# Norm factors behind the first products, first weights in halves, and a feed loop that splits its first loads

## The chip, the cores and the metric

The program runs on one core of a Trainium2 chip. The metric is the device time of one execution in microseconds, lower being better. The time given for a kernel is the median of its runs.

## The reference, cut to what matters

A sequence of 256 tokens with 1024 features passes through two layers and a second block. Layer 0 is retention and a squared-ReLU MLP, layer 1 an attention that selects blocks (here there is one block) and an MLP. The second block has four parallel branches under gates, a cross attention to a memory, and a gated feed-forward part. Each part reads `rms_norm(h, g_pre)` and adds `rms_norm(part(...), g_post)` to `h`.

```python
def rms_norm(x, g):
    xf = x.astype(jnp.float32)
    y = xf * lax.rsqrt(jnp.mean(xf * xf, axis=-1, keepdims=True) + NORM_EPS)
    return (y * g.astype(jnp.float32)).astype(x.dtype)
...
    q, k, v, g = jnp.split(h @ w_in, [H * DK, 2 * H * DK, 2 * H * DK + H * DV], axis=-1)
...
    o = o * lax.rsqrt(jnp.mean(o * o, axis=-1, keepdims=True) + NORM_EPS)
    o = o.transpose(0, 2, 1, 3).reshape(B, S, H * DV)
    o = o * jax.nn.silu(g.astype(jnp.float32))
    return o.astype(h.dtype) @ w_out
...
    for i in range(DEPTH):
        pre, post, w_in, w_out, mpre, mpost, w_up, w_down = layers[i]
        h = h + rms_norm(mixers[i % N_MIXERS](rms_norm(h, pre), w_in, w_out), post)
        h = h + rms_norm(sq_relu_mlp(rms_norm(h, mpre), w_up, w_down), mpost)
```

## The kernel before, in words

All weights are float32 and stream from memory once, as 203 chunks of 1 MB in the order of their use. A chunk comes in two pieces of 128x1024 (512 KB), which makes 406 pieces. Float32 products are made of float32r ones: a piece that has landed (`raw`) is split into `whi` (ScalarE, a copy, L156) and `wlo` (VectorE, the difference, L162), the activations into `xhi` and `xlo`, and `mm3` (L235 to L237) issues three products for each k-tile: hi by hi, hi by lo of the weights, lo by hi. The second of the three is the first that needs `wlo`.

The work of TensorE is cut into units. One unit takes one chunk with one token tile of 128 (there are two, t0 and t1) and is 12 products of 128x512, six on the chunk's first piece and six on its second; or it takes one chunk with all tokens and 24 products of 128x256. Behind each unit stands a call of `tick(n)`: it starts the split of up to n pieces (`prepare`), lets the background work (attention heads, activations) take one step, finishes the splits, and calls `feed()`, which issues loads on SyncE's queue until `nraw` pieces (5, and 3 at the end of a layer) are loaded ahead of their split. A piece counts as ready for a split two ticks after its load was issued, and at most `nprep` pieces (11 to 13) may be split ahead. If a unit comes to a chunk whose pieces have not been split, `weights()` splits them on the spot (`prepare(force=True)`).

The order of the program is the order of these calls; nothing is rescheduled. Every engine works its own instructions in that order and waits for what is not there yet.

At the end of each part stands `boundary`. Its last products take token tile 0 first, so that the norms of tile 0 run under the products of tile 1, and the norms of tile 1 under the next part's four (or three) units of token tile 0 (`fill0`). These units call `tick(2 * t)` with t = 0, so that they start no splits: in this stretch ScalarE and VectorE have the norm chain of tile 1, the evacuations of the units, and the transposed `xhi` and `xlo` of tile 1. U1, U2, U3 and U4 below are these four units in order; in front of U4 stand the transposes of tile 1.

There are five such boundaries with as_group units behind them: retention to MLP 0, MLP 0 to the block attention, that to MLP 1, MLP 1 to the second block, and cross attention to the feed-forward part. A sixth leads from the branches to the cross attention.

In front, `prenorm(h[0], g0, ...)` makes the normed tile 0 in token-major form, `to_T` transposes it on TensorE and splits it into `xhi` and `xlo`, and the first unit follows. The gain `gain_first` is loaded as a 128x1024 tile, the same row on all partitions.

These are the lines around which the change turns:

```python
    def feed(n=None):
        n = n or state["nraw"]
        while state["dma"] < min(npiece, state["prep"] + n):
            raw = b4([128, 1024], "raw")
            nc.sync.dma_start(raw, wall[state["dma"]])
            raws[state["dma"]] = raw, state["now"] + 2
            state["dma"] += 1
```

Of the kernel before, what the change touches and what calls it, by code (L numbers as in the profile page):

```python
# [24 lines left out]
# Newton steps for 1/sqrt on a scaled iterate: z -> (z*z*x - 3*c*c)*z maps c*y to -2*c^3*y'.  # L25
# [3 lines left out]
# columns of w_in_2  # L29
# [7 lines left out]
# columns of the per-partition parameter array  # L37
# [7 lines left out]
# columns of the row parameter array  # L45
# [21 lines left out]
    # retention rotary, transposed: [freq, pos]  # L67
# [4 lines left out]
    # partial rope, natural: [pos in tile, tile, cos cos | sin -sin]  # L72
# [15 lines left out]
# tiles of 4 KB a partition, for weights and data  # L88
NB4 = 43
# pieces that are loaded ahead of their split, and split ahead of their use, at the end of a layer  # L90
AHEAD = 3, 16
# products of the last layer behind its last activations
TAIL = 4
# pieces of weights that are split ahead, by phase
# [5 lines left out]
def tile_model(ctx: ExitStack, tc: tile.TileContext, order, wall, x, mem, gains, pparam, rparam, w_fg,  # L100
# [27 lines left out]
    # Chunks of 1 MB in the order of their use, in two pieces of 1024 columns. A piece lies in SBUF as loaded, and  # L128
    # then as two float32r parts, hi and lo, whose sum is the float32 value.
# [4 lines left out]
    def feed(n=None):  # L134
        n = n or state["nraw"]
        while state["dma"] < min(npiece, state["prep"] + n):
            raw = b4([128, 1024], "raw")
            nc.sync.dma_start(raw, wall[state["dma"]])
            raws[state["dma"]] = raw, state["now"] + 2
            state["dma"] += 1  # L140

    def waiting():
        """Pieces that can be split now: loads that were issued at least two ticks ago."""
        end = min(state["dma"], 2 * state["done"] + state["nprep"])
        return sum(raws[i][1] <= state["now"] for i in range(state["prep"], end))

    def prepare(n=1, force=False):
        """Start to split n pieces; the function that is returned does the rest of it."""
# [18 lines left out]
    def weights(key):  # L167
        """The two parts of the next chunk, each in two pieces."""
# [35 lines left out]
    def later(f):  # L204
        """Call f within the next tick but one."""
# [13 lines left out]
    def pipe(n, *stages, wait=0):  # L219
        """Stages (delay, f) of n items, one item a step; the later stages of earlier items go first."""  # L220
# [18 lines left out]
    def ws(o, w, c0, xh, xl, width=256):  # L239
        """o[feature, token] = w^T x; the chunk is [128][2048 / width][width]."""  # L240
# [5 lines left out]
    def as_(o, w, xh, xl, t, start, stop):  # L246
        """o[token, 512] += x w over the 4 k-tiles of a chunk [128][4][512]."""
# [5 lines left out]
    def down(acc, w, ah, al, t, start, stop):  # L253
        """acc[token, 1024] += a w over the 2 k-tiles of a chunk [128][2][1024]."""
# [18 lines left out]
    def rstd(ss, w, inv_d, name):  # L273
        """1/sqrt(ss*inv_d + eps), elementwise on [128, w]."""
# [28 lines left out]
    h = [cp.tile([128, D], F32, name=f"h{t}") for t in range(2)]  # L303
    HS = [slice(0, 512), slice(512, 1024)]
    g0 = b4([128, D], "gain_first")
    for t in range(2):
        for n in range(2):
            nc.sync.dma_start(h[t][:, HS[n]], x[0, tok(t), HS[n]])
        if t == 0:
            for n in range(2):  # L310
                nc.sync.dma_start(g0[:, HS[n]], gains[0:1, HS[n]].broadcast_to([128, 512]))
        feed(4 * t + 2)
# [12 lines left out]
    # the layer's input, transposed, in two parts of four k-tiles each  # L325
# [21 lines left out]
    def rms_scale(src, g, y, name):  # L347
        """y = src * g; returns 1/sqrt(mean(src^2) + eps), by ScalarE's square root and a Newton step in x' = 4x.
        Sources and results are pairs of halves."""
# [24 lines left out]
    def chain(acc, gp, gn, t, name, store=False, between=None):  # L374
        """h[t] += rms_norm(acc, gp); returns rms_norm(h[t], gn)."""
# [11 lines left out]
    def prenorm(src, gn, y, name):  # L387
        """y = rms_norm(src, gn)"""
# [51 lines left out]
    def as_group(specs, xh=xh2, xl=xl2):  # L440
        """specs: (keys of the two chunks, evacuate(t, psum)). Work of token tile 0, work of token tile 1."""
# [32 lines left out]
    def ws_units(key, evac, xh=xh, xl=xl, n=None):  # L474
        """The work of one chunk in two units."""
# [33 lines left out]
    def ret_vg_specs(hd):  # L509
# [3 lines left out]
        evacs = (lambda t, ps: split(rv[hd][0][:, t, :], rv[hd][1][:, t, :], ps),  # L513
                 lambda t, ps: nc.scalar.activation(rg[hd][:, t, :], ps, AF.Silu))
# [15 lines left out]
    def ret_attn(hd):  # L530
# [3 lines left out]
        for jt in range(2):  # L534
            o = ps[:, 0:256] if jt == 0 else ps[:, 256:384]
            for f in range(2):
                nc.tensor.matmul(o, qkT[:, 2 + f, tok(jt)], qkT[:, f, jt * 128:256], start=f == 0, stop=f == 1)
        pt = t2("pt")
        nc.vector.tensor_tensor(pt[:, 0:384], ps[:, 0:384], dec[hd // 2][:, (hd % 2) * 384:(hd % 2) * 384 + 384],
                                op=ALU.mult)  # L540
# [5 lines left out]
        for t in range(2):  # L546
# [5 lines left out]
            nc.scalar.activation(og, po, AF.Square, accum_out=ss)  # L552
            r = rstd(ss, 1, 1.0 / 512, "ret")
            nc.vector.scalar_tensor_tensor(og, po, r, g[:, t, :], op0=ALU.mult, op1=ALU.mult)
# [23 lines left out]

    load_sqrt()
    xn = prenorm(h[0], g0, b4([128, D], "xn0"), "f0")  # L580
    prepare(1, force=True)()
    new_x()
    to_T(xn, 0, xh2, xl2)
    prepare(1, force=True)()
    specs = ret_vg_specs(0)
    fill = as_group(specs[:1])
    fill[0][0]()
    prepare(2, force=True)()
    xn = b4([128, D], "xn1")
    r = rms_scale(two(h[1]), None, None, "f1")()  # L590
    for n in range(2):
        nc.vector.scalar_tensor_tensor(xn[:, HS[n]], h[1][:, HS[n]], r, g0[:, HS[n]], op0=ALU.mult, op1=ALU.mult)
    fill[0][1]()
    to_T(xn, 1, xh2, xl2)
    for f in fill[1]:
        f()
# [33 lines left out]
    def mlp_start(i):  # L630
        """The first 1024 features with tokens on the partitions, so that token tile 0 can go first."""
# [118 lines left out]
    def moba_n(hd):  # L750
        p = mp[hd]
        b, l, rl = mst.pop(hd)
        # the selected block is never a past one: each of its 256 weights is exp(NEG - m)
# [821 lines left out]
```

## Time and profile before

| what | value |
|---|---|
| time, median of 3 runs | 1275.82 us (1275.37 to 1276.14) |
| profiled execution, span | 1274.1 us |
| lies around the span, against the median | 1.7 us |
| TensorE busy | 1251.6 us, 98% of the span |
| VectorE busy | 877.6 us, 69% |
| ScalarE busy | 680.0 us, 53% |
| DMA | 227.43 MB, 179 GB/s |

The span is that of the profiled execution, the time that of runs without a profile. Busy times are means over a span with parts that have different limits; VectorE and ScalarE are far from full over the whole, and what they are at a given place is to be read there.

### The profile page before, as it was taken

How to read it: one execution, taken by the hardware profiler on the slowest of the kernel's cores; microseconds unless marked ns; L12 is line 12 of the kernel's file. 1: busy time of each engine (PE TensorE's matmuls, PEld its weight loads, DVE VectorE, ACT ScalarE, POOL GpSimd, SP SyncE). 2: the span in 40 equal slices, each digit the busy share in tenths (PEclk: the TensorE clock that was granted, in tenths of full speed). 3: DMA queues.
4: the chain of work that ended last, by engine and by line, in shares of the span. 5: the costliest groups of instructions: out<-in, count | busy, mean ns of one | idle time of the engine just before them, and what ended most of it. 6: DMA issues, size and time to landing. Idle time of an engine off the chain costs nothing.

```text
span 1274.1 us, 20056 instructions
## 1 busy us (share of the span) xinstructions
PE 1251.6 (98%) x7886; PEld 1123.7 (88%) x7886; DVE 877.6 (69%) x1540; ACT 680.0 (53%) x1104; POOL 9.3 (1%) x22
## 2 busy tenths in 40 slices
PE   6999999999999999999999999999999999999997
PEld 4888888899988888899988999889999897899996
DVE  5775768755556866765566677768877877588773
ACT  5553445644444755654453546555346565666552
POOL 0000000000000000000000000000000000000000
PEclk9999999999999999999999999999999999999999
DMA  9754464665564545566664644235566564465530
GB/s 346 270 186 158 153 226 154 215 203 185 183 207 150 183 136 176 182 210 188 196 202 163 215 133 149 67 118 180 183 182 203 190 220 165 150 191 185 187 116 34
DMA packets 64206, 227.43 MB, mean 179 GB/s; under 512 B 8048, under 2 KB 8304, under 8 KB 64112
## 3 DMA queue, kind: packets, MB, share of 16 engines
q1 hardware_dynamic: 61808, 217.76, 52.0%
q0 software_dynamic: 2304, 8.39, 1.9%
q8 instruction: 62, 1.02, 0.3%
q14 instruction: 32, 0.26, 0.1%
HBM read 225.08 MB, written 1.05 MB: 177 GB/s over the span
## 4 chain that ended last, share of the span: by engine, by line
PE 95%; DVE 2%; ACT 1%; issue 1%; DMA 1%; SPq 0%; DVEq 0%; ACTq 0%
PE ps_ws L235 13%; PE ps_ws L237 13%; PE ps_ws L236 13%; PE ps_as L237 6%; PE ps_as L235 6%; PE ps_as L236 6%; PE mlp L268 4%; PE mlp L267 4%; PE mlp L271 4%; PE ffn L268 1%; PE ffn L271 1%; PE ffn L267 1%; PE ps_br L235 1%; PE ps_br L237 1%; PE ps_br L236 1%; PE pt L294 1%
## 5 line engine op out<-in xcount | busy, mean ns | idle before, releaser
L162 DVE TENSOR_TENSOR wlo<-raw,whi 128x1024 fp32r<-128x1024 f32 x406 | 480.0, 1219 | 78.5 <-ACT whi L156 77.3
L156 ACT ACTIVATE whi<-raw 128x1024 fp32r<-128x1024 f32 x406 | 406.7, 1049 | 53.8 <-PE ps_ws L237 15.4
L235 PE MATMUL ps_ws<-xhi,whi 128*128 128x256 f32 x1376 | 391.6, 285 | 0.0
L236 PE MATMUL ps_ws<-xlo,whi 128*128 128x256 f32 x1376 | 389.3, 283 | 0.0
L237 PE MATMUL ps_ws<-xhi,wlo 128*128 128x256 f32 x1376 | 389.3, 283 | 0.0
L235 PEld LDWEIGHTS ps_ws<-xhi,whi 128*128 128x128 f32 x1376 | 263.8, 192 | 5.2 <-issue 3.7
L236 PEld LDWEIGHTS ps_ws<-xlo,whi 128*128 128x128 f32 x1376 | 263.9, 192 | 1.5
L237 PEld LDWEIGHTS ps_ws<-xhi,wlo 128*128 128x128 f32 x1376 | 263.8, 192 | 0.0
L235 PE MATMUL ps_as<-whi,xhi 128*128 128x512 f32 x352 | 142.6, 405 | 0.3 <-ACT xhi L231 0.2
L237 PE MATMUL ps_as<-whi,xlo 128*128 128x512 f32 x352 | 138.4, 393 | 0.1
L236 PE MATMUL ps_as<-wlo,xhi 128*128 128x512 f32 x352 | 138.1, 392 | 0.0
L268 PE MATMUL mlp<-wlo,act 128*128 128x512 f32 x240 | 93.7, 390 | 0.0
L267 PE MATMUL mlp<-whi,act 128*128 128x512 f32 x240 | 93.5, 390 | 0.0
L237 PEld LDWEIGHTS ps_as<-whi,xlo 128*128 128x128 f32 x352 | 66.4, 189 | 15.5 <-DVE xlo L232 1.2
L235 PEld LDWEIGHTS ps_as<-whi,xhi 128*128 128x128 f32 x352 | 66.6, 189 | 13.8 <-ACT xhi L231 1.1
L236 PEld LDWEIGHTS ps_as<-wlo,xhi 128*128 128x128 f32 x352 | 66.6, 189 | 13.6 <-DVE wlo L162 0.8
L662 DVE SCALAR_TENSOR_TENSOR relu<-ps_ws,relu 128x512 f32<-128x512 f32 x24 | 16.6, 691 | 87.1 <-ACT relu L661 87.1
L661 ACT ACTIVATE relu<-ps_ws 128x512 f32<-128x512 f32 x24 | 14.4, 598 | 113.8 <-PE ps_ws L237 113.8
L271 PE MATMUL mlp<-whi,act 128*128 128x512 f32 x240 | 74.0, 389 | 0.0
L271 PEld LDWEIGHTS mlp<-whi,act 128*128 128x128 f32 x240 | 45.1, 188 | 9.6
L268 PEld LDWEIGHTS mlp<-wlo,act 128*128 128x128 f32 x240 | 45.2, 188 | 8.6
L267 PEld LDWEIGHTS mlp<-whi,act 128*128 128x128 f32 x240 | 45.2, 188 | 8.6
(426 smaller groups left out, 1637.4 us busy)
## 6 DMA issues: line engine op xcount, KB each, us to landing
raw<-in_wall_dram SPq DMA_DIRECT2D x406, 512.0 KB, 4.1
h<-in_x_dram SPq DMA_DIRECT2D x4, 256.0 KB, 6.0
gainln_mix_post<-in_gains_dram POOLq DMA_DIRECT2D x2, 512.0 KB, 5.0
gainln_mlp_pre<-in_gains_dram POOLq DMA_DIRECT2D x2, 512.0 KB, 5.6
gainln_mlp_post<-in_gains_dram POOLq DMA_DIRECT2D x2, 512.0 KB, 7.1
mem<-in_mem_dram POOLq DMA_DIRECT2D x2, 512.0 KB, 5.9
out_dram<-h SPq DMA_DIRECT2D x4, 256.0 KB, 2.0
dec<-in_t_dec_dram SPq DMA_DIRECT2D x2, 384.0 KB, 8.9
```

The lines of the kernel that those rows point to most:

```text
L156: nc.scalar.activation(hi, raw, AF.Copy)
L162: nc.vector.tensor_tensor(lo, raw, hi.bitcast(F32), op=ALU.subtract)
L235: nc.tensor.matmul(o, ah, bh, start=start, stop=False)
L236: nc.tensor.matmul(o, ah, bl, start=False, stop=False)
L237: nc.tensor.matmul(o, al, bh, start=False, stop=stop)
L267: nc.tensor.matmul(acc[t][n], ah[:, k, ts], wh[k][:, ns], start=st, stop=False)
L268: nc.tensor.matmul(acc[t][n], ah[:, k, ts], wl[k][:, ns], start=False, stop=False)
L271: nc.tensor.matmul(acc[t][n], al[:, k, ts], wh[k][:, ns], start=False, stop=False)
L294: nc.tensor.transpose(dst[:, k * 128:k * 128 + 128], src[:, k * 128:k * 128 + 128], ident)
L661: nc.scalar.activation(r, ps, AF.Relu)
L662: nc.vector.scalar_tensor_tensor(r, ps, 0.0, r, op0=ALU.max, op1=ALU.mult)
```

## The change

The head of layer 0 is written anew. The first layer's inputs are transposed as they come, without their norm; the gain, now a 128x8 tile with one column for each k-tile, is applied where the transposed tile is split (`first_x`: 16 pairs of a 128x128 ScalarE copy with a scale and a VectorE instruction). The norm factor of each token, `r0[t]`, is worked out while the products run and applied behind them: in the evacuation of v and g, in the decay of the scores and in the inner norm of the retention. Pieces 0 and 1 are loaded as two halves each and split in halves (`prepare_halves`). Five products of the identity with itself stand in front. The order of the first units is t0 chunk 0, t1 chunk 0, t0 chunk 1, t1 chunk 1, where it was t0 chunk 0, t0 chunk 1, t1 chunk 0, t1 chunk 1.

```diff
     def feed(n=None):
         n = n or state["nraw"]
         while state["dma"] < min(npiece, state["prep"] + n):
             raw = b4([128, 1024], "raw")
-            nc.sync.dma_start(raw, wall[state["dma"]])
+            parts = 2 if state["dma"] < 2 else 1
+            for n in range(parts):
+                sl = slice(n * (1024 // parts), (n + 1) * (1024 // parts))
+                nc.sync.dma_start(raw[:, sl], wall[state["dma"]][:, sl])
             raws[state["dma"]] = raw, state["now"] + 2
             state["dma"] += 1
 
+    def prepare_halves():
+        i = state["prep"]
+        state["prep"] += 1
+        raw, _ = raws.pop(i)
+        hi, lo = ready[i] = b4([128, 1024], "whi", F32R), b4([128, 1024], "wlo", F32R)
+        for n in range(2):
+            sl = slice(n * 512, n * 512 + 512)
+            yield
+            nc.scalar.activation(hi[:, sl], raw[:, sl], AF.Copy)
+            nc.vector.tensor_tensor(lo[:, sl], raw[:, sl], hi[:, sl].bitcast(F32), op=ALU.subtract)
+        yield
...
-        evacs = (lambda t, ps: split(rv[hd][0][:, t, :], rv[hd][1][:, t, :], ps),
-                 lambda t, ps: nc.scalar.activation(rg[hd][:, t, :], ps, AF.Silu))
+        def value(t, ps):
+            nc.scalar.activation(rv[hd][0][:, t, :], ps, AF.Copy, scale=r0[t])
+            nc.vector.scalar_tensor_tensor(rv[hd][1][:, t, :], ps, r0[t], rv[hd][0][:, t, :].bitcast(F32),
+                                           op0=ALU.mult, op1=ALU.subtract)
...
-        nc.vector.tensor_tensor(pt[:, 0:384], ps[:, 0:384], dec[hd // 2][:, (hd % 2) * 384:(hd % 2) * 384 + 384],
-                                op=ALU.mult)
+        for jt, sl in enumerate((slice(0, 256), slice(256, 384))):
+            c0 = (hd % 2) * 384 + sl.start
+            nc.vector.scalar_tensor_tensor(pt[:, sl], ps[:, sl], r0[jt], dec[hd // 2][:, c0:c0 + sl.stop - sl.start],
+                                           op0=ALU.mult, op1=ALU.mult)
...
+            nc.vector.tensor_tensor(r, r, r0[t], op=ALU.mult)
...
+    def first_x(t, q, pt):
+        for k in range(4):
+            src, g = pt[:, k * 128:k * 128 + 128], g0[:, 4 * q + k:4 * q + k + 1]
+            hi, lo = xh2[q][:, k, tok(t)], xl2[q][:, k, tok(t)]
+            nc.scalar.activation(hi, src, AF.Copy, scale=g)
+            nc.vector.scalar_tensor_tensor(lo, src, g, hi.bitcast(F32), op0=ALU.mult, op1=ALU.subtract)
...
+    warm = bank("warm")
+    for _ in range(5):
+        nc.tensor.matmul(warm[:, 0:128], ident, ident, start=True, stop=True)
     new_x()
-    to_T(xn, 0, xh2, xl2)
-    prepare(1, force=True)()
+    first = [prepare_halves(), prepare_halves()]
...
+    feed()
     specs = ret_vg_specs(0)
     fill = as_group(specs[:1])
     fill[0][0]()
+    for q in range(2):
+        first_x(1, q, first_T(1, q))
     prepare(2, force=True)()
...
+    for t in range(2):
+        r0.append(rms_scale(two(h[t]), None, None, f"f{t}")())
+    fill[1][0]()
     fill[0][1]()
-    to_T(xn, 1, xh2, xl2)
-    for f in fill[1]:
-        f()
+    fill[1][1]()
     as_pair(*specs[1])
```

The loop over the parts of a load in `feed` has the name `n`, which is also the name of the argument that the `while` above it reads.

The first place is SyncE's queue at the start of the program, where the loads are issued. Before:

```order
L308 DMA h_72<-in_x_dram 128x512 x2
L311 DMA gain_first<-in_gains_dram 128x512 x2
L138 DMA raw<-in_wall_dram 128x1024 x2
L308 DMA h_73<-in_x_dram 128x512 x2
L138 DMA raw<-in_wall_dram 128x1024 x4
L498 DMA rot<-in_t_rot_dram 128x1024
```

The same place with the change:

```order
L322 DMA h_72<-in_x_dram 128x512
L323 DMA gain_first<-in_gain_dram 128x8
L324 DMA h_72<-in_x_dram 128x512
L141 DMA raw<-in_wall_dram 128x512 x2
L327 DMA h_73<-in_x_dram 128x512 x2
L141 DMA raw<-in_wall_dram 128x512 x2
L514 DMA rot<-in_t_rot_dram 128x1024
L516 DMA dec_98<-in_t_dec_dram 128x768
L516 DMA dec_99<-in_t_dec_dram 128x768
L141 DMA raw<-in_wall_dram 128x1024
```

Where six pieces were loaded ahead of `rot`, two now are (each in two halves), and one behind the decay tables, where four calls of `feed` ask for 2, 6, 5 and 5 pieces.

The second place is ScalarE in the head, before:

```order
L353 ACTIVATE sqj,sf_117<-h_72 128x512 x2
L358 ACTIVATE sf_117<-sf_117 128x1
L156 ACTIVATE whi<-raw 128x1024
L231 ACTIVATE xhi<-pt 128x4x128 x2
L156 ACTIVATE whi<-raw 128x1024 x3
L353 ACTIVATE sqj,f_189<-h_73 128x512 x2
L358 ACTIVATE f_189<-f_189 128x1
L231 ACTIVATE vh<-ps_as 128x512
```

and with the change, with what each waits for (DVE_49 is VectorE's counter, PE_49 TensorE's, the DMAHW ones loads):

```order
L615 ACTIVATE xhi<-pt,gain_first 128x128 [waits DMAHW1_49,PE_49]
L615 ACTIVATE xhi<-pt,gain_first 128x128 [waits DVE_49] x3
L154 ACTIVATE whi<-raw 128x512 [waits DMAHW3_49]
L154 ACTIVATE whi<-raw 128x512 [waits DMAHW4_49]
L615 ACTIVATE xhi<-pt,gain_first 128x128 [waits PE_49]
L615 ACTIVATE xhi<-pt,gain_first 128x128 [waits DVE_49] x3
L154 ACTIVATE whi<-raw 128x512 [waits DMAHW7_49]
L154 ACTIVATE whi<-raw 128x512 [waits DMAHW0_49]
L615 ACTIVATE xhi<-pt,gain_first 128x128 [waits PE_49]
L615 ACTIVATE xhi<-pt,gain_first 128x128 [waits DVE_49] x3
L615 ACTIVATE xhi<-pt,gain_first 128x128 [waits PE_49]
L615 ACTIVATE xhi<-pt,gain_first 128x128 [waits DVE_49] x3
```

The norm's squares have moved behind the first products, and of the four copies for one transposed bank the last three each wait for VectorE, which reads the same bank in between.

The third place is ScalarE at the boundary from retention to MLP 0 (`s` is the norm factor of token tile 1, `relu` the evacuation of U2 and then U4, `act` the split of what U2 made, `xhi` that of tile 1's input). Before:

```order
L353 ACTIVATE sqj,s_2075<-h_73 128x512 x2
L358 ACTIVATE s_2075<-s_2075 128x1
L636 ACTIVATE relu<-ps_as 128x512
L231 ACTIVATE act<-ps_at 128x2x128 x2
L231 ACTIVATE xhi<-pt 128x4x128 x2
L636 ACTIVATE relu<-ps_as 128x512
```

The same place with the change:

```order
L369 ACTIVATE sqj,s_2072<-h_73 128x512 x2
L374 ACTIVATE s_2072<-s_2072 128x1
L172 ACTIVATE whi<-raw 128x1024
L684 ACTIVATE relu<-ps_as 128x512
L172 ACTIVATE whi<-raw 128x1024 x2
L247 ACTIVATE act<-ps_at 128x2x128 x2
L247 ACTIVATE xhi<-pt 128x4x128 x2
L172 ACTIVATE whi<-raw 128x1024 x2
L684 ACTIVATE relu<-ps_as 128x512
```

Five splits of weights now stand here where none stood: of U2's second piece, of both of U3 and of both of U4, each by the `force` in `weights()`. VectorE's five `wlo` stand in its order at the same places, behind what the ScalarE rows have in front of them.

## Rows read from the trace of the kernel before

**Rows 1.** Page: busy time (share of the span) of TensorE, and its granted clock.
```profile
PE 1251.6 (98%) x7886; PEld 1123.7 (88%) x7886; DVE 877.6 (69%) x1540; ACT 680.0 (53%) x1104; POOL 9.3 (1%) x22
...
PEclk9999999999999999999999999999999999999999
```
**Rows 2.** Page, costliest groups: the two halves of a split.
```profile
L162 DVE TENSOR_TENSOR wlo<-raw,whi 128x1024 fp32r<-128x1024 f32 x406 | 480.0, 1219 | 78.5 <-ACT whi L156 77.3
L156 ACT ACTIVATE whi<-raw 128x1024 fp32r<-128x1024 f32 x406 | 406.7, 1049 | 53.8 <-PE ps_ws L237 15.4
```
**Rows 3.** Waits of 0 to 40 us: us in total, times, longest.
```profile
PE pt L294 <- DVE xn L391: 11.2, 1, 11.2
```
**Rows 4.** TensorE's timeline in the head: start us, us, instruction.
```profile
13.00 0.79 PE L235 MATMUL ps_as<-whi,xhi 128*128 128x512 f32 x1
...
14.45 0.63 PE L235 MATMUL ps_as<-whi,xhi 128*128 128x512 f32 x1
14.88 0.63 PE L236 MATMUL ps_as<-wlo,xhi 128*128 128x512 f32 x1
...
16.91 0.39 PE L235 MATMUL ps_as<-whi,xhi 128*128 128x512 f32 x1
...
27.65 0.39 PE L235 MATMUL ps_as<-whi,xhi 128*128 128x512 f32 x1
```
**Rows 5.** ScalarE's timeline in the head; in brackets idle time before, and its end.
```profile
4.32 0.63 ACT L353 ACTIVATE sqj<-h 128x512 f32<-128x512 f32 x1 [0.21 <-DMA h<-in_x_dram]
...
27.85 0.60 ACT L231 ACTIVATE vh<-ps_as 128x512 fp32r<-128x512 f32 x1 [3.73 <-PE ps_as L237]
```
**Rows 6.** ScalarE's timeline at the boundary from retention to MLP 0.
```profile
216.65 0.30 ACT L358 ACTIVATE s<-s 128x1 f32<-128x1 f32 x1
217.79 0.60 ACT L636 ACTIVATE relu<-ps_as 128x512 f32<-128x512 f32 x1 [0.85 <-PE ps_as L237]
220.95 0.39 ACT L231 ACTIVATE act<-ps_at 128x256 fp32r<-128x256 f32 x1 [2.56 <-PE ps_at L294]
221.83 0.39 ACT L231 ACTIVATE act<-ps_at 128x256 fp32r<-128x256 f32 x1 [0.49 <-DVE act L232]
222.11 1.08 ACT L231 ACTIVATE xhi<-pt 128x512 fp32r<-128x512 f32 x2
```
**Rows 7.** VectorE's timeline at the same boundary.
```profile
217.80 0.88 DVE L391 TENSOR_SCALAR y<-y,s 128x512 f32<-128x512 f32 x2
218.60 0.68 DVE L637 SCALAR_TENSOR_TENSOR relu<-ps_as,relu 128x512 f32<-128x512 f32 x1
...
222.74 1.29 DVE L232 TENSOR_TENSOR xlo<-pt,xhi 128x512 fp32r<-128x512 f32 x2
```
**Rows 8.** TensorE's timeline at the same boundary: starts of U2, U3, transposes, U4.
```profile
214.87 0.39 PE L235 MATMUL ps_as<-whi,xhi 128*128 128x512 f32 x1
...
217.59 0.39 PE L235 MATMUL ps_as<-whi,xhi 128*128 128x512 f32 x1
...
220.32 0.60 PE L294 MATMUL ps_at<-ident,relu 128*128 128x128 f32 x4
...
221.55 0.48 PE L235 MATMUL ps_as<-whi,xhi 128*128 128x512 f32 x1
```
**Rows 9.** Groups by form, ScalarE: a 128x128 instruction with a scale from a tile.
```profile
L887 ACT ACTIVATE cxn<-ps_ct,pp 128x128 f32<-128x128 f32 x8 | 2.9, 465 | 0.0
```
**Rows 10.** TensorE's timeline: U3 and U4 to the second block, U2 to the feed-forward.
```profile
693.36 0.39 PE L235 MATMUL ps_as<-whi,xhi 128*128 128x512 f32 x1
...
696.88 0.48 PE L235 MATMUL ps_as<-whi,xhi 128*128 128x512 f32 x1
...
1081.89 0.39 PE L235 MATMUL ps_as<-whi,xhi 128*128 128x512 f32 x1
```
**Rows 11.** VectorE's timeline at these two boundaries.
```profile
693.56 0.88 DVE L391 TENSOR_SCALAR y<-y,s 128x512 f32<-128x512 f32 x2
...
1085.32 0.88 DVE L391 TENSOR_SCALAR y<-y,s 128x512 f32<-128x512 f32 x2
```
**Rows 12.** ScalarE's timeline at the boundary to the second block.
```profile
693.56 0.60 ACT L831 ACTIVATE av<-ps_as 128x512 f32<-128x512 f32 x1 [0.85 <-PE ps_as L237]
696.72 1.09 ACT L231 ACTIVATE xhi<-pt 128x512 fp32r<-128x512 f32 x2 [2.56 <-PE pt L294]
```

More of the change, by code (lines that the diff above doesn't have):

```diff
@@ L99, in tile_model @@
 @with_exitstack
-def tile_model(ctx: ExitStack, tc: tile.TileContext, order, wall, x, mem, gains, pparam, rparam, w_fg,
+def tile_model(ctx: ExitStack, tc: tile.TileContext, order, wall, x, mem, gains, gain0, pparam, rparam, w_fg,
                t_dec, t_rot, t_small, out, upto=99):
@@ L304, in tile_model @@
     HS = [slice(0, 512), slice(512, 1024)]
[L305 to L312, printed above, removed]
+    g0 = cp.tile([128, 8], F32, name="gain_first")
+    nc.sync.dma_start(h[0][:, HS[0]], x[0, tok(0), HS[0]])
+    nc.sync.dma_start(g0, gain0)
+    nc.sync.dma_start(h[0][:, HS[1]], x[0, tok(0), HS[1]])
+    feed(2)
+    for n in range(2):
+        nc.sync.dma_start(h[1][:, HS[n]], x[0, tok(1), HS[n]])
+    feed(6)
     ident = cp.tile([128, 128], F32, name="ident")
@@ L511, in ret_vg_specs @@
         rg[hd] = b4([128, 2, 512], "g")
-        evacs = (lambda t, ps: split(rv[hd][0][:, t, :], rv[hd][1][:, t, :], ps),
-                 lambda t, ps: nc.scalar.activation(rg[hd][:, t, :], ps, AF.Silu))
+        def value(t, ps):
+            nc.scalar.activation(rv[hd][0][:, t, :], ps, AF.Copy, scale=r0[t])
+            nc.vector.scalar_tensor_tensor(rv[hd][1][:, t, :], ps, r0[t], rv[hd][0][:, t, :].bitcast(F32),
+                                           op0=ALU.mult, op1=ALU.subtract)
+        evacs = (value, lambda t, ps: nc.scalar.activation(rg[hd][:, t, :], ps, AF.Silu, scale=r0[t]))
         return [([("ret_vg", nm, hd, c) for c in range(2)], evacs[nm]) for nm in range(2)]
@@ L551, in ret_attn @@
             ss = stat("ss_ret", 1)
-            nc.scalar.activation(og, po, AF.Square, accum_out=ss)
+            nc.scalar.activation(og, po, AF.Square, scale=r0[t], accum_out=ss)
             r = rstd(ss, 1, 1.0 / 512, "ret")
+            nc.vector.tensor_tensor(r, r, r0[t], op=ALU.mult)
             nc.vector.scalar_tensor_tensor(og, po, r, g[:, t, :], op0=ALU.mult, op1=ALU.mult)
@@ L577, in ret_out, with first_T @@
         del roT[hd]
+    r0 = []
+    def first_T(t, q):
+        pt = bank("pt")
+        transposes(pt, h[t][:, HS[q]])
+        return pt
+    def first_x(t, q, pt):
[4 more added lines that the diff above has]
+            nc.vector.scalar_tensor_tensor(lo, src, g, hi.bitcast(F32), op0=ALU.mult, op1=ALU.subtract)
     load_sqrt()
-    xn = prenorm(h[0], g0, b4([128, D], "xn0"), "f0")
-    prepare(1, force=True)()
+    warm = bank("warm")
+    for _ in range(5):
+        nc.tensor.matmul(warm[:, 0:128], ident, ident, start=True, stop=True)
     new_x()
-    to_T(xn, 0, xh2, xl2)
-    prepare(1, force=True)()
+    first = [prepare_halves(), prepare_halves()]
+    for f in first:
+        next(f)
+    pts = [first_T(0, q) for q in range(2)]
+    first_x(0, 0, pts[0])
+    next(first[0])
+    next(first[0])
+    first_x(0, 1, pts[1])
+    next(first[1])
+    next(first[1])
+    feed()
     specs = ret_vg_specs(0)
@@ L587, in tile_model @@
     fill[0][0]()
+    for q in range(2):
+        first_x(1, q, first_T(1, q))
     prepare(2, force=True)()
[L589 to L592, printed above, removed]
+    for t in range(2):
+        r0.append(rms_scale(two(h[t]), None, None, f"f{t}")())
+    fill[1][0]()
     fill[0][1]()
-    to_T(xn, 1, xh2, xl2)
-    for f in fill[1]:
-        f()
+    fill[1][1]()
     as_pair(*specs[1])
@@ L1548, in build @@
     dec, rot, small = shape_tables()
-    arrays = {"x": inp["x"], "mem": inp["mem_2"], "gains": gains, "pparam": pparam, "rparam": rparam,
+    arrays = {"x": inp["x"], "mem": inp["mem_2"], "gains": gains, "gain0": gains[0].reshape(8, 128).T, "pparam": pparam, "rparam": rparam,
               "w_fg": w_fg, "t_dec": dec, "t_rot": rot, "t_small": small}
@@ L1557, in build @@
     with tile.TileContext(nc) as tc, tc.manual_schedule():
-        tile_model(tc, order, wall, aps["x"], aps["mem"], aps["gains"], aps["pparam"], aps["rparam"], aps["w_fg"],
+        tile_model(tc, order, wall, aps["x"], aps["mem"], aps["gains"], aps["gain0"], aps["pparam"], aps["rparam"], aps["w_fg"],
                    aps["t_dec"], aps["t_rot"], aps["t_small"], out, upto=upto)
```

## The prediction

> **What bounds the kernel now.** I read the page first. TensorE is busy for 98% of the span at the full granted clock [rows 1], so the program is a row of products with few holes, and a change can gain only what is left of the holes. The waits of the first 40 us show the one large hole: TensorE stands for 11.2 us until the norm of token tile 0 is there [rows 3]. The timeline then gives the first product at 13.00, products 0.43 us apart (14.45 to 14.88) until about 16.9, 0.23 us apart from there, and the first chunk of the second pair at 27.65 [rows 4]. That is the place the change is written for, and at most some 9 us lie there.
>
> Then I looked for what the other engines do when the products have no hole. A piece takes ScalarE 1.05 us and VectorE 1.22 us [rows 2], a unit of 12 products takes TensorE 2.72 us (214.87 to 217.59) [rows 8]. Two pieces, one chunk, are 2.1 and 2.44 us, just inside a unit; what a unit needs beyond that must have been split earlier. So the reserve of split pieces is what keeps the products dense, and it is spent at the layer boundaries, where the units of token tile 0 start no splits. At the first boundary the timelines show ScalarE and VectorE on the norm of tile 1 and on evacuations (s at 216.65, y at 217.80, relu, act, xhi, xlo) while U2, U3 and U4 run with no gap between them [rows 6 to 8]. There is no split in that stretch, because the pieces were ready.
>
> **The change, part by part.** *The feed loop.* The inner `for n in range(parts)` overwrites the argument. After the first load n is 0 (or 1), the `while` asks for `dma < prep + 0`, and it ends. Every call of `feed` therefore issues one load at most, whatever it was asked for; the SyncE rows in the section on the change show it, three pieces where seven were asked for ahead. With a tick that may split two pieces and a feed that brings one, and a piece that counts as ready only two ticks after its load, the reserve never grows to `nprep`. Following the calls through the program, the pieces split ahead at a chunk's use fall from 10 to 12 down to 4 in the retention and 7 later, and raw pieces ahead from 5 to 2 or 3. Off the boundaries that is enough: a unit still finds its pieces, and data land long before the split, so I cost these stretches at nothing; the cover is the 4 to 7 pieces, each worth half a unit, 1.4 us. At the boundaries it is not enough: twelve units there (three at two boundaries, two at three) have pieces that are split only when the unit asks for them.
>
> *Price of a late split.* The second product of a k-tile needs `wlo`. A unit whose both pieces are late waits for the first `wlo` at its 2nd product, 0.23 us after its start; one whose second piece is late at its 8th, 7 x 0.227 = 1.59 us after it. The second late piece comes 1.22 us behind the first, while six products take 1.36 us, so it adds nothing.
>
> Retention to MLP 0: piece 67, U2's second, stands on VectorE behind y, which ends at 218.63 (the relu starts at 218.60) [rows 7]. `wlo` ends at 219.85; the 8th product was due at 214.87 + 1.59 = 216.46 [rows 8]: 3.4 us. U3's pieces stand behind its predecessor's relu on ScalarE: 0.2 us after U2's end the relu (0.60) starts [rows 6, 8], then `whi` 1.05 and `wlo` 1.22, together 3.07 behind U2's end where 0.23 was due: 2.85. U4's stand behind act and xhi, which ends at 223.19, 1.64 us after U4's start at 221.55 [rows 6, 8]; `whi` 2.69, `wlo` 3.91 after it, due 0.23: 3.7. Sum 10.0.
>
> MLP 0 to the attention and MLP 1 to the second block are alike, read at the latter: U3's second piece stands behind y (693.56 + 0.88 = 694.44) and a copy of 0.60 with `whi` behind it (695.2) [rows 11, 12], so `wlo` ends at 696.4, due 693.36 + 1.59 = 694.95 [rows 10]: 1.45. U4: xhi ends at 697.81, 0.93 after U4's start [rows 10, 12], so `wlo` at about 3.2, due 0.23: 3.0. Sum 4.45 each. Attention to MLP 1: both U3 and U4 as at the first boundary, 2.85 + 3.7 = 6.55. Cross attention to feed-forward: y ends at 1086.20 [rows 11], `wlo` 1087.42, due 1081.89 + 1.59 = 1083.48 [rows 10]: 3.9, then 2.85 and 3.0: 9.75. The five boundaries: 10.0 + 4.45 + 6.55 + 4.45 + 9.75 = 35.2. Since each of these is a gap between engines with some tenths of its own, I put it at 31 to 39.
>
> *The head.* h's second half lands at 4.3 [rows 5]; transposes take 0.4 to 0.6 (a row like 220.32) [rows 8]. Then come four pairs of ScalarE and VectorE for each bank, and the rows of the order show that each copy waits for VectorE's read of the pair before. The nearest row for such an alternation is the two act splits, 0.88 us from start to start at 256 columns [rows 6]; the nearest for one 128x128 link on ScalarE alone is 0.465 us [rows 9]. I take 0.8, near the first, for both stand in a chain: 3.2 us for each of the four banks. So first product at about 8.0 (4.3 + 0.5, 3.2 for the chain with `whi` behind it), 5 us earlier than 13.00. But the unit then waits for the second bank and piece 1, and ends near 14.5. Tile 1's two banks follow in series, to 21.9; only behind them stand `whi` and `wlo` of pieces 2 and 3, to 24.9; t0's second unit ends near 27, t1's near 30.5, where the old order reached 27.65 [rows 4]. Pieces 4 to 7 stand on ScalarE behind tile 1's v, which waits for that end (27.85 in the old run) [rows 5]; the old run had pieces 4 and 5 before it. Four `wlo` at 1.22 pace the next two units, so that their end moves from 33.1 to about 38. Head: +5. Bounds: -1, if the links take 0.47, to +7.
>
> *The rest.* The retention's reserve of 4 is short by a fraction of a split at the four pairs of units where attention also runs: 0 to 4 us (four times one split less a little), I take 2. The extra VectorE work (a second multiplication for the scores, factors at the norms, some tenths of a us each) hides under products. Branches to cross attention: two pieces late by up to one `wlo` each, 0 to 2.5, taken 1.3. Start of the feed-forward: 0 to 6, taken 1, since several pieces of its thin reserve are each near the edge.
>
> *The five idle products.* TensorE was idle until 12.11 or so, and eight transposes just ahead of the first product left it at 0.43 us [rows 3, 4]. Five small products near 1 us, then idle until 5, I therefore cost at nothing; the products of the head run at 0.43 for their first microseconds, as now. The Trainium skill, "TensorE: Matmul & The Clock Gate" ("Why this matters for your kernels"), advises to warm the array with products before what counts. By that the head would be up to 8 x 0.2 = 1.6 us shorter, and the sum 1318 and not 1320.
>
> **Sum.** 35.2 + 5 + 2 + 1.3 + 1 = 44.5 on a span of 1274.1, that is 1318.6; with the 1.7 us that lie around the span, 1320.
>
> **The rivals.** *Faster.* The change does what its words say: the first product comes 5.0 us earlier and all else hides, 1270.8. For it speaks the 11.2 us wait [rows 3]. It decides if the late splits and the later head together cost under 5 us. Against it: five `whi` stand at the first boundary in ScalarE's order where none stood, and the rows leave no slack there.
>
> *The clock falls.* After its long wait TensorE starts at 0.43 us a product [rows 3, 4]. If waits of 1.5 to 4 us did the same, each late unit would pay up to 12 x 0.2 = 2.4 us more: 12 x 2.4 = 28.8, or 1349. The trace of before has no wait of that size behind dense products, so rows leave it open; that the cold start followed a wait three times as long speaks against it. The same page of the Trainium skill says that an array left idle returns to the lower of its two clock levels (1.2 and 2.4 GHz); which of these waits would do it, no run here shows.
>
> *Half the price.* If a late unit waits only for what ScalarE has to do (its order lets `whi` go ahead), and VectorE catches up within the unit, the boundaries cost about half, 17.6, and the head 2: with the rest 1298.
>
> *No change.* Gains in the head would have to cancel the boundaries: a split reserve larger than I count, by chance.
>
> **How the numbers follow.** Forecast 0.73, clock 0.10, half 0.12, faster 0.03, no change 0.02. The forecast's own range adds its bounds: -1 + 31 = 30 to 7 + 39 + 4 + 2.5 + 6 = 58.5, so 1306 to 1334. The range for 8 in 10 reaches halfway into the two neighbours: 1298 to 1346. A measurement of this kernel can tell 0.2%, 2.5 us, from no change. Slower takes in forecast, clock and half: 0.95; faster 0.03; within 0.2% 0.02.
>
> **What would show it.** In the profile after: five boundaries with TensorE waiting for VectorE's `wlo`, 3.4, 2.85 and 3.7 us at the first; ScalarE with `whi` between relu and act there; the first product near 8, chunk 4's start 5 us later than now; PEclk full except in the head. Wrong would be: waits for raw data in place of `wlo` (loads late, then the price is a transfer, not a split), or TensorE waiting in the middle of phases, where I put nothing.

## The result and the profile after

The changed kernel takes 1336.17 us (median of 4 runs, 1330.01 to 1338.74) where the kernel before takes 1275.6 us: a ratio of 1.0468, 95% interval 1.0446 to 1.0491, or some 60 us slower. The forecast was 1320 us, in a range of 1298 to 1346. Each time below has the kernel before measured beside it, at 1275.2 to 1275.8 us; ratios and their 95% intervals are to that.

The page after: span, busy time, and granted clock in tenths by slices (the page is that of an execution of 1334.0 us).

```profile
span 1332.1 us, 20044 instructions
...
PE 1279.8 (96%) x7896; PEld 1135.5 (85%) x7896; DVE 881.0 (66%) x1560; ACT 683.4 (51%) x1118; POOL 9.3 (1%) x22
...
PEclk7999999999999999899999999999999999899999
```

Against [rows 1], the span is 58.0 us longer and TensorE is busy 28.2 us longer with nearly the same products. So 30 us are time in which TensorE stands, and 28 us are time in which it counts as busy for longer. Not all of the 28 is the clock, though three slices are no longer at 9: 7.5 us lie in the head, and 18.6 at the five boundaries, where a product that stands alone between two waits also counts longer (0.50 us in the row at 227.44 below, where the next product of a dense row starts after 0.23). What the clock costs is told by e4. What TensorE stands for is in the list of waits (us in total, times, longest):

```profile
PE ps_as L251 <- ACT whi L172: 23.2, 14, 2.6
PE ps_as L252 <- DVE wlo L178: 11.9, 17, 1.4
PE ps_as L251 <- ACT whi L154: 3.1, 2, 1.9
```

The one wait of 11.2 us for the norm [rows 3] is gone, and waits for splits have come, 14 for a `whi` and 17 for a `wlo` behind pieces 0 and 1. Twelve of each lie at the five boundaries, one of each for each of the twelve late units: the first product that needs the late piece waits for its `whi`, and the next one for its `wlo`. At the boundary from retention to MLP 0 the timeline of TensorE shows them (in brackets the wait before and its end); the rows answer to [rows 8]:

```profile
224.37 0.39 PE L251 MATMUL ps_as<-whi,xhi 128*128 128x512 f32 x1
...
227.44 0.50 PE L251 MATMUL ps_as<-whi,xhi 128*128 128x512 f32 x1 [1.54 <-ACT whi L172]
229.36 0.50 PE L252 MATMUL ps_as<-wlo,xhi 128*128 128x512 f32 x1 [1.43 <-DVE wlo L178]
...
232.40 0.80 PE L251 MATMUL ps_as<-whi,xhi 128*128 128x512 f32 x1 [1.63 <-ACT whi L172]
233.66 0.80 PE L252 MATMUL ps_as<-wlo,xhi 128*128 128x512 f32 x1 [0.46 <-DVE wlo L178]
...
234.67 0.63 PE L251 MATMUL ps_as<-whi,xhi 128*128 128x512 f32 x1
235.10 0.63 PE L252 MATMUL ps_as<-wlo,xhi 128*128 128x512 f32 x1
...
238.30 0.60 PE L310 MATMUL ps_at<-ident,relu 128*128 128x128 f32 x4
...
242.16 0.50 PE L251 MATMUL ps_as<-whi,xhi 128*128 128x512 f32 x1 [2.40 <-ACT whi L172]
243.42 0.50 PE L252 MATMUL ps_as<-wlo,xhi 128*128 128x512 f32 x1 [0.76 <-DVE wlo L178]
```

U2 starts at 224.37; its 8th product was due 1.59 us later, at 225.96, and starts at 229.36: 3.40 us late. U3's second was due at 230.84 (0.23 behind its first, which was due at 230.61) and starts at 233.66: 2.8. U4 was due 1.23 us behind the start of the transposes, its second product at 239.76, and starts it at 243.42: 3.7. But from 234.25 to 237.66 the products stand 0.43 us apart (234.67, 235.10), not 0.23.

ScalarE at the same place, for [rows 6], and below it VectorE, for [rows 7]: the splits lie where the order had put them, between s, relu and xhi.

```profile
226.14 0.29 ACT L374 ACTIVATE s<-s 128x1 f32<-128x1 f32 x1
226.34 1.04 ACT L172 ACTIVATE whi<-raw 128x1024 fp32r<-128x1024 f32 x1
230.80 0.60 ACT L684 ACTIVATE relu<-ps_as 128x512 f32<-128x512 f32 x1 [3.42 <-PE ps_as L253]
231.30 1.99 ACT L172 ACTIVATE whi<-raw 128x1024 fp32r<-128x1024 f32 x2
...
241.04 2.02 ACT L172 ACTIVATE whi<-raw 128x1024 fp32r<-128x1024 f32 x2
```

```profile
227.29 0.88 DVE L407 TENSOR_SCALAR y<-y,s 128x512 f32<-128x512 f32 x2
228.09 1.22 DVE L178 TENSOR_TENSOR wlo<-raw,whi 128x1024 fp32r<-128x1024 f32 x1
```

No split here waits for a transfer: each `whi` starts as soon as the instruction ahead of it on ScalarE is done, and each `wlo` behind its `whi` and the instruction ahead of it on VectorE.

The head, TensorE and then ScalarE, for [rows 4, 5]:

```profile
8.07 0.50 PE L251 MATMUL ps_as<-whi,xhi 128*128 128x512 f32 x1 [1.87 <-ACT whi L154]
...
22.61 0.49 PE L251 MATMUL ps_as<-whi,xhi 128*128 128x512 f32 x1 [2.60 <-ACT whi L172]
...
33.87 0.51 PE L251 MATMUL ps_as<-whi,xhi 128*128 128x512 f32 x1 [1.72 <-ACT whi L172]
```

```profile
4.77 0.37 ACT L615 ACTIVATE xhi<-pt,gain_first 128x128 fp32r<-128x128 f32 x1 [2.53 <-PE pt L310]
5.56 0.37 ACT L615 ACTIVATE xhi<-pt,gain_first 128x128 fp32r<-128x128 f32 x1 [0.42 <-DVE xlo L616]
...
32.19 0.69 ACT L530 ACTIVATE vh<-ps_as,f 128x512 fp32r<-128x512 f32 x1 [2.53 <-PE ps_as L253]
32.78 3.89 ACT L172 ACTIVATE whi<-raw 128x1024 fp32r<-128x1024 f32 x4
```

The first product does come at 8.07 instead of 13.00. Then the copies of `first_x` come 0.79 us apart, each behind VectorE's read; t0's second unit waits for pieces 2 and 3 until 22.6; and pieces 4 to 7 stand behind tile 1's v on ScalarE, so that the next pair of chunks starts at 33.87, not 27.65.

To place the loss, I took the last product of each stretch in both timelines and the difference of the two starts; what a stretch adds is the growth of that difference. The first column names the product's start before and after.

| stretch, its last product (before, after) | forecast | after | e2 | e4 | e1 |
|---|---|---|---|---|---|
| head (38.59, 45.71) | 5.0 | 7.1 | 5.2 | 7.6 | 3.9 |
| retention (208.30, 217.81) | 2.0 | 2.4 | 1.5 | 2.4 | 0.0 |
| to MLP 0 (226.89, 248.58) | 10.0 | 12.2 | 17.0 | 10.2 | 0.0 |
| to the attention (409.09, 435.37) | 4.45 | 4.6 | 6.3 | 4.7 | 0.0 |
| to MLP 1 (520.46, 557.57) | 6.55 | 10.8 | 10.8 | 6.6 | 0.0 |
| to the second block (710.34, 753.64) | 4.45 | 6.2 | 6.2 | 4.6 | 0.0 |
| branches to cross attention (1019.10, 1063.77) | 1.3 | 1.4 | 1.7 | 1.4 | 0.0 |
| to the feed-forward (1093.91, 1151.93) | 9.75 | 13.35 | 13.3 | 10.0 | 0.0 |
| rest | 1.0 | 0.0 | 0.0 | 0.0 | 0.0 |
| sum | 44.5 | 58.0 | 61.9 | 47.5 | 3.9 |

The columns e1, e2 and e4 are the experiments below, each against the kernel before.

### The profile page after: what moved, and what is told of

It is laid out like the page before. It is cut to its first block, busy times and chain, and to the rows that moved or that the text cites. A ratio compares the mean times of both kernels' runs of the same rounds, so it can differ in the third digit from the quotient of the medians.

```text
span 1332.1 us, 20044 instructions
## 1 busy us (share of the span) xinstructions
PE 1279.8 (96%) x7896; PEld 1135.5 (85%) x7896; DVE 881.0 (66%) x1560; ACT 683.4 (51%) x1118; POOL 9.3 (1%) x22
## 4 chain that ended last, share of the span: by engine, by line
PE 86%; DVE 7%; ACT 4%; DMA 1%; issue 1%; SPq 0%; DVEq 0%; ACTq 0%
PE ps_ws L251 12%; PE ps_ws L252 12%; PE ps_ws L253 12%; PE ps_as L252 6%; PE ps_as L253 5%; PE ps_as L251 5%; PE mlp L284 4%; PE mlp L283 4%; PE mlp L287 4%; DVE wlo L178 3%; ACT whi L172 2%; DMA raw<-in_wall_dram 1%; PE ffn L284 1%; PE ffn L283 1%; PE ffn L287 1%
## 5 line engine op out<-in xcount | busy, mean ns | idle before, releaser
L172 ACT ACTIVATE whi<-raw 128x1024 fp32r<-128x1024 f32 x404 | 403.6, 1049 | 0.1
L251 PE MATMUL ps_as<-whi,xhi 128*128 128x512 f32 x352 | 149.8, 425 | 26.6 <-ACT whi L172 23.2
L252 PE MATMUL ps_as<-wlo,xhi 128*128 128x512 f32 x352 | 145.9, 415 | 12.1 <-DVE wlo L178 11.9
L253 PE MATMUL ps_as<-whi,xlo 128*128 128x512 f32 x352 | 144.0, 409 | 0.0
L251 PEld LDWEIGHTS ps_as<-whi,xhi 128*128 128x128 f32 x352 | 69.6, 198 | 47.2 <-ACT whi L172 28.4
L252 PEld LDWEIGHTS ps_as<-wlo,xhi 128*128 128x128 f32 x352 | 69.9, 198 | 32.5 <-DVE wlo L178 18.1
L253 PEld LDWEIGHTS ps_as<-whi,xlo 128*128 128x128 f32 x352 | 69.9, 198 | 15.4 <-DVE xlo L248 0.4
```

What stands on the lines that cost most here:

```text
L172: nc.scalar.activation(hi, raw, AF.Copy)
L251: nc.tensor.matmul(o, ah, bh, start=start, stop=False)
L252: nc.tensor.matmul(o, ah, bl, start=False, stop=False)
L253: nc.tensor.matmul(o, al, bh, start=False, stop=stop)
```

## The experiments

The theory (A): the lost argument of `feed` thins the reserve of split pieces, and this is the whole loss behind the head; the head has its own, from the serial copies and from the order on ScalarE. The rival (B): the new arithmetic behind the products fills ScalarE and VectorE, so that splits come late. A second question: the 13.5 us by which the trace lies beyond the forecast (58.0 against 44.5), is it the clock?

**e1, feed repaired.** In the changed kernel, the inner loop gets a name of its own.

```diff
-            for n in range(parts):
-                sl = slice(n * (1024 // parts), (n + 1) * (1024 // parts))
+            for part in range(parts):
+                sl = slice(part * (1024 // parts), (part + 1) * (1024 // parts))
```

> The changed kernel with the inner loop of feed under a name of its own, so that a feed loads as many pieces as it is asked for. Theory A (the lost name is the whole loss behind the head): the boundaries and the retention fall back to the kernel before, and what stays is the head. There 4 us stay of the 7.1: the serial chain of first_x, but not the 3.1 us for pieces 4 and 5, which now stand ahead of v. Time 1278 to 1281. Theory B (the new arithmetic behind the products thins the reserve of split pieces on ScalarE and VectorE): most of the loss stays, above 1315.

Measured: 1280.44 us (1279.28 to 1281.27), ratio 1.0039, interval 1.0025 to 1.0054. Behind the head nothing is left: the difference is 3.92 us at the end of the head and 3.88 at the feed-forward. B falls. The one lost name costs some 56 of the 60 us (1336.17 against 1280.44). In the head, TensorE's waits of the first 45 us hold none for pieces 4 and 5 any more; what stays are two for pieces 0 and 1 (L154) and one for pieces 2 and 3 (L172):

```profile
PE ps_as L251 <- ACT whi L154: 3.9, 2, 2.4
PE ps_as L251 <- ACT whi L172: 2.2, 1, 2.2
```

**e2, only the lost argument.** The kernel before, with one line at the end of the loop in `feed`.

```diff
             state["dma"] += 1
+            n = 0
```

> The kernel before with one line more: feed sets n to 0 after its first load, so that it issues one load a call. Theory A: the five boundaries lose what they lose in the changed kernel, 45 to 50 us, the retention 2 or so, and the head as pieces 4 to 7 come later, 0 to 4: 1322 to 1332. Theory B: the same as before within 5 us, 1276 to 1281.

Measured: 1336.46 us (1333.42 to 1338.49), ratio 1.0478, interval 1.0462 to 1.0493. One load a call, with nothing else of the change, is as slow as the whole change; the time lies above the expectation's upper end by 4 us, and the table shows where: at the boundary to MLP 0 it adds 17.0, with 24 of its products there 0.43 us apart, where the changed kernel has 8. The head loses 5.2, where 0 to 4 were expected, although its norms are as before: pieces 2 and 3 are loaded late, and ScalarE waits 2.8 and 3.2 us for their landing.

**e3, copies first.** e1, and in `first_x` all four copies of a bank ahead of the four differences.

```diff
-        for k in range(4):
-            src, g = pt[:, k * 128:k * 128 + 128], g0[:, 4 * q + k:4 * q + k + 1]
-            hi, lo = xh2[q][:, k, tok(t)], xl2[q][:, k, tok(t)]
+        part = [(pt[:, k * 128:k * 128 + 128], g0[:, 4 * q + k:4 * q + k + 1], xh2[q][:, k, tok(t)], xl2[q][:, k, tok(t)])
+                for k in range(4)]
+        for src, g, hi, lo in part:
             nc.scalar.activation(hi, src, AF.Copy, scale=g)
+        for src, g, hi, lo in part:
             nc.vector.scalar_tensor_tensor(lo, src, g, hi.bitcast(F32), op0=ALU.mult, op1=ALU.subtract)
```

> e1 with the four copies of a bank issued ahead of its four differences, so that no copy waits for VectorE. If the alternation (0.79 us a link in the trace of the changed kernel) sets the head: each of the four banks is done 1.3 to 1.5 us sooner, and the time is 4 to 5.5 us under e1, 1274 to 1276. If the head is set by the arrival of pieces 1 and 2 and by the slow clock: within 1 us of e1.

Measured: 1273.73 us (1271.53 to 1274.16), ratio 0.9984, interval 0.9975 to 0.9993: 6.7 us under e1, and faster than the kernel before. ScalarE's timeline shows four copies in 1.14 us, where three links took 2.36 (4.77 to 7.13) in the changed kernel:

```profile
4.76 1.14 ACT L615 ACTIVATE xhi<-pt,gain_first 128x128 fp32r<-128x128 f32 x4 [2.52 <-PE pt L310]
...
14.22 2.18 ACT L615 ACTIVATE xhi<-pt,gain_first 128x128 fp32r<-128x128 f32 x8 [3.67 <-PE pt L310]
```

So the alternation set the head. The gain is over the expected 4 to 5.5 us; the wait of 2.2 us for pieces 2 and 3 is gone, and t0's second unit also stays at 0.23 us a product, where e1 has eight at 0.43. The second row shows the next hole: ScalarE stands 3.67 us until tile 1's transposes, and after that it is full. In the row of the stretch from 14 to 24 us, TensorE's busy time is the first pair of figures behind the length (us, instructions), and ScalarE's the fourth:

```profile
14.00:24.00 10.00, 9.38 (x42) 7.00 (x41) 7.34 (x22) 9.28 (x23) 0.00 (x0) 1.00 1.05 383
```

In this trace a first product 6.4 us earlier (6.57 against 13.00) gives only 3.1 us at the end of the head. The full ScalarE has a small part in that, since TensorE itself is busy for 9.38 of these 10 us. Most of it is lost in the first unit, whose twelve products take 7.0 us up to tile 1's transposes, where the kernel before takes 4.6 (13.00 to 17.61): they wait for halves of pieces, and nearly all come at 0.43 us or more.

```profile
6.57 0.79 PE L251 MATMUL ps_as<-whi,xhi 128*128 128x512 f32 x1 [0.31 <-ACT whi L154]
...
13.58 1.04 PE L310 MATMUL pt<-ident,h 128*128 128x128 f32 x8
```

**e4, products of zeros in the waits.** The changed kernel with its late splits; in the late units of the boundaries, small products that add zeros while TensorE would stand. The lines that choose the units and their counts are left out.

```diff
...
+            if idle and k == idle[0]:
+                zero = small[:, C_MASK:C_MASK + 128]
+                for _ in range(idle[1]):
+                    nc.tensor.matmul(o[:, 0:128], zero, ident, start=st, stop=st)
+                nc.tensor.matmul(o, xh[:, k, ts], wh[k], start=st, stop=False)
+                for _ in range(idle[2]):
+                    nc.tensor.matmul(o[:, 0:128], zero, ident, start=False, stop=False)
...
```

> The changed kernel with its late splits, and in the late units of the five boundaries products of a 128x128 zero with the identity while TensorE would wait (7 ahead of the first weights, 4 ahead of wlo; 3 and 2 where the wait is short). They add zeros to the result. If the time beyond the waits for whi and wlo is the granted clock at half in the units behind a wait: TensorE stays at the full clock there and 6 to 13 us come back, 1322 to 1330. If the clock falls all the same, or the loss is in the waits alone: 1334 to 1342.

Measured: 1323.36 us (1323.10 to 1323.51), ratio 1.0377, interval 1.0362 to 1.0391: 13 us under the changed kernel by the medians and 10.5 in the traces (47.5 against 58.0 in the table), with more work. The page's granted clock has no low slice, and TensorE's timeline at the same boundary shows U3's products 0.23 us apart behind the same wait:

```profile
PEclk9999999999999999999999999999999999999999
```

```profile
232.89 0.50 PE L271 MATMUL ps_as<-whi,xhi 128*128 128x512 f32 x1
233.22 1.05 PE L273 MATMUL ps_as<-ident,small 128*128 128x128 f32 x8
234.15 0.50 PE L274 MATMUL ps_as<-wlo,xhi 128*128 128x512 f32 x1
234.49 0.40 PE L275 MATMUL ps_as<-whi,xlo 128*128 128x512 f32 x1
234.72 0.39 PE L251 MATMUL ps_as<-whi,xhi 128*128 128x512 f32 x1
```

The splits are as late as before, and nothing else is lost at the boundaries: each of them adds what the forecast's rows gave for the waits alone (10.2, 4.7, 6.6, 4.6, 10.0 against 10.0, 4.45, 6.55, 4.45, 9.75). The scatter says the same: the changed kernel's runs spread over 8.7 us, with a mean granted clock of 0.985 in the fastest and 0.981 in the slowest, those of e4 over 0.4 us.

The last five ask what the rest of the change is worth, from e3 on. The runs of e3 alone spread over 2.6 us, so differences of less than 1 us among these kernels can't be told.

**e5, no idle products**: e3 without the five products of the identity.

> e3 without the five products of the identity. If they do nothing for the clock of the first unit (its products are 0.43 us apart in e1 and e3 with them): the same as e3 within 1 us, 1273 to 1275. If they bring the rise of the clock forward: 1.5 to 3 us over e3, 1275 to 1277.

Measured: 1272.66 us, ratio 0.9977 (0.9968 to 0.9987), e3's being 0.9984 (0.9975 to 0.9993). The intervals share most of their length: no gain from the idle products shows.

**e6, whole pieces**: e3 with pieces 0 and 1 loaded and split whole.

> e3 with pieces 0 and 1 loaded and split whole. The first unit needs the first half of a piece for its first three products; whole, whi of piece 0 waits for the landing of the second half (7.85 in the trace of e3) and takes 1.05 instead of 0.63, so the first product comes at 9 instead of 6.57. If the first unit's end sets the head: 1 to 2.5 us over e3, 1275 to 1276. If later work of ScalarE and VectorE sets it: within 1 us of e3.

Measured: 1273.37 us, ratio 0.9983 (0.9974 to 0.9992): no difference from e3. The first product comes at 7.88 instead of 6.57 (9 was expected), but the first unit ends only 0.4 us later (14.00 against 13.58): with whole pieces it waits less inside. That later work on ScalarE and VectorE sets the head, as the expectation's second branch says, isn't shown by this.

**e7, the old order of the units**: e3, and

```diff
     fill[0][0]()
+    prepare(2, force=True)()
     for q in range(2):
         first_x(1, q, first_T(1, q))
-    prepare(2, force=True)()
...
-    fill[1][0]()
     fill[0][1]()
+    fill[1][0]()
     fill[1][1]()
```

> e3 with the order of the first units as before (t0 chunk 0, t0 chunk 1, t1 chunk 0, t1 chunk 1) and pieces 2 and 3 split ahead of tile 1's input. If ScalarE's 3.67 us without work until tile 1's transposes (10.5 to 14.2 in e3) are what costs: whi 2 and 3 fill it, and the time is 1 to 2 us under e3, 1271.5 to 1272.7. If pieces 2 and 3 have not landed by then, ScalarE waits for them with tile 1's input behind: 1 to 3 us over e3.

Measured: 1271.04 us (1270.92 to 1272.44), ratio 0.9965, interval 0.9953 to 0.9978. That is 2.4 us under e3 by the ratios, though the two intervals still touch; in the traces it is 0.9 us (4.0 us under the kernel before at the end of the head, against 3.1; the trace of e7 is of its slowest run). The order and the place of the splits were changed together, and the run doesn't part them. ScalarE now has the splits of pieces 2 and 3 in its hole, behind a wait for their landing:

```profile
11.69 1.06 ACT L172 ACTIVATE whi<-raw 128x1024 fp32r<-128x1024 f32 x1 [1.37 <-DMA raw<-in_wall_dram]
12.98 1.06 ACT L172 ACTIVATE whi<-raw 128x1024 fp32r<-128x1024 f32 x1 [0.23 <-DMA raw<-in_wall_dram]
14.49 2.17 ACT L615 ACTIVATE xhi<-pt,gain_first 128x128 fp32r<-128x128 f32 x8 [0.46 <-PE pt L310]
```

**e8, piece 1 first**: e3 with piece 1 split ahead of tile 0's second bank.

> e3 with piece 1 split ahead of the second bank of tile 0's input, which the first unit does not read. The first unit waits 1.04 us for whi of piece 1 in e3. If that wait counts: 0.5 to 1 us under e3, 1272.7 to 1273.2. If the units behind are paced by ScalarE and VectorE anyway: the same as e3 within 0.4 us.

Measured: 1272.53 us, ratio 0.9974 (0.9964 to 0.9985): lower than e3, but not by more than the intervals allow. Inconclusive.

**e9, together**: e7 with the edits of e5 and e8.

> e7 with piece 1 split ahead of tile 0's second bank (as in e8) and without the products of the identity (as in e5). In e7 TensorE still waits 1.0 us for whi of piece 1 and 1.0 us for wlo in the first unit. If the edits add up: 0.5 to 1.5 us under e7, 1269.5 to 1270.5. If the landing of pieces 2 and 3 (ScalarE waits for them at 11.7 in e7) sets the units behind: the same as e7 within 0.4 us.

Measured: 1270.81 us (1270.49 to 1271.23), ratio 0.9964 (0.9951 to 0.9978), the same as e7, which agrees with the landing of pieces 2 and 3 as the limit (ScalarE waits for it at 12.11 here), but doesn't prove it. With e7 this is the fastest version: 4.4 us under the kernel before.

## Why the prediction was right, and where its size was off

**The step that carried it.** The reading of `feed` was right: e1 and e2 show that the lost argument alone makes the late splits, and that without it nothing is left behind the head. The stretches that were costed at nothing added nothing, and the late units number twelve.

**The price of a late split** was right unit by unit: 3.4, 2.85 and 3.7 us forecast at the first boundary, 3.40, 2.8 and 3.7 measured; and over the five boundaries 35.2 forecast against 36.1 in e4, where the clock is held.

**The term that was mis-sized is the clock**, costed at nothing in the forecast and set aside as a rival ("that the cold start followed a wait three times as long speaks against it"). It fell at four of the five boundaries: about 12 us there, 47.2 measured against 35.2. The rival itself, 2.4 us in each of twelve late units, was too much: at the boundary to the attention no product was slow, and at the others one or two units were. So the truth lay between the two: 1336.17 is 2 us above the forecast's own 1306 to 1334 and nearer to the rival's 1349 than to 1320, and it lies in the stated range because that range took in part of the rival. Waits as short as these do lower the clock, but not each time. At the boundary to the attention the same two waits left the products 0.23 us apart in the changed kernel, and 0.43 in e2, where seven products are slow (first the changed kernel, then e2):

```profile
428.99 0.50 PE L251 MATMUL ps_as<-whi,xhi 128*128 128x512 f32 x1 [1.73 <-ACT whi L172]
430.25 0.50 PE L252 MATMUL ps_as<-wlo,xhi 128*128 128x512 f32 x1 [0.76 <-DVE wlo L178]
...
430.82 0.39 PE L251 MATMUL ps_as<-whi,xhi 128*128 128x512 f32 x1
431.05 0.40 PE L252 MATMUL ps_as<-wlo,xhi 128*128 128x512 f32 x1
```

```profile
430.99 0.51 PE L236 MATMUL ps_as<-whi,xhi 128*128 128x512 f32 x1 [1.73 <-ACT whi L157]
432.25 0.50 PE L237 MATMUL ps_as<-wlo,xhi 128*128 128x512 f32 x1 [0.76 <-DVE wlo L163]
...
432.86 0.63 PE L236 MATMUL ps_as<-whi,xhi 128*128 128x512 f32 x1
433.29 0.63 PE L237 MATMUL ps_as<-wlo,xhi 128*128 128x512 f32 x1
```

What tells the two apart stays open. In the changed kernel the lowest granted clock reads 0.50, which is 1.2 GHz; the row is that of the boundary to the feed-forward, busy time of TensorE first and the clock third from the end:

```profile
1138.00:1142.00 4.00, 4.00 (x11) 3.08 (x10) 0.33 (x1) 0.00 (x0) 0.00 (x0) 0.50 0.00 0
```

Eleven products in 4 us, all at 0.43 us, after four products in the 4 us before. The Trainium skill, "TensorE: Matmul & The Clock Gate" ("HAM oscillation — how this bites in real kernels"), says that waits between short bursts of products bring the lower clock back each time they are long enough, so that the products behind a wait run slow. The trace agrees in kind, with 0.50 in the row above; the rows of the boundary to the attention show that the length of the waits alone did not decide it here.

**The head**: the links were right (0.8 forecast, 0.79 measured), as were the first product (8.0 and 8.07) and the end of tile 1's chain (21.9 and 22.0). The 2.1 us beyond the forecast come mostly from t0's second unit and the start of t1's: the products from 24.5 to 29.6 stand 0.43 us apart after the wait that ends at 22.61, where I had let the full clock go on, and t1's second unit ends at 32.0, not 30.5. It is the same step. The next pair ends at 40.5 where 38 was forecast, so some of the difference lies there.

**The idle products** at nothing: right (e5), though not for the reason given. They run from 1.36 us until the first transposes at 3.66, so TensorE was not idle until 5, as the prediction had it; the first unit ran at 0.43 us all the same. The Trainium skill, "TensorE: Matmul & The Clock Gate" ("Why this matters for your kernels"), advises to warm up with products first; the 1.6 us that the prediction set beside this did not come, and products that reach up to the first unit were not tried. **Retention** 2 against 2.4 (four waits for a `wlo`) and **branches to cross attention** 1.3 against 1.4 (two): right. **Start of the feed-forward** 1 against 0: its reserve was enough.

**Half the price** fell by e4, with 36.1 us at the boundaries and not 17.6; its sum should have read 1299.7 and not 1298, since it left out the 1.7 us around the span. **No change** and **faster** by the result. Faster was what the words of the change promise, and e3 shows it was in reach: the head's idea gains 2 us by the ratio once the feed loads and the copies don't alternate, and 4.5 in the old order of the units (e7).

## What to carry to other kernels

A reserve that is filled by a loop is worth a count of what it holds at each place, not only in the mean: here the loads behind the head still came in time, VectorE and ScalarE were idle for a third and half of the span, and a dozen units with late splits cost 47 us. A wait of TensorE costs its own length and then, sometimes, more in products at the lower clock (here between nothing and some two thirds of the waits of a boundary: 4.2 us on 6.6 on the way to MLP 1); whoever prices a wait should carry both. Two engines that split one bank in small pieces should each get their pieces in a row, since an order written as copy, difference, copy, difference made a chain of 0.79 us a link out of copies that take 0.28 us each in a row.

## What the runs showed of the hardware that was not expected

Waits of at most 2.4 us, with one to a few products between them, lowered the clock at four boundaries and left it at a fifth, where e2 had it fall behind the same waits. The changed kernel's runs differ by 8.7 us, and those of e4, where the waits are filled, by 0.4. And the granted clock of a stretch does not show every slow product: in the head of the kernel before it reads 1.00 from 13 to 17 us, while the products of that stretch stand 0.43 us apart [rows 4]. The row of its windows:

```profile
13.00:17.00 4.00, 4.00 (x11) 2.91 (x11) 3.59 (x4) 3.79 (x5) 0.00 (x0) 1.00 1.02 406
```

The pitch of the products is the surer sign.
